# RWKV scan: the triangular solve made ahead of the chunk steps, and the state's product added per direction

## Chip, cores and metric

One core of a Trainium2 chip runs the whole program. The metric is the device time of one execution in microseconds (us); less is better.

## The reference, cut to what matters

The program is two transformer blocks; the second one's later mixer is an RWKV layer that runs forward and backward over 256 context and 512 latent positions with 16 heads of 64:

```python
def _wkv_step(S, inp):
    r_t, w_t, k_t, v_t, a_t, b_t = inp
    sa = jnp.einsum('zbhvk,zbhk->zbhv', S, a_t)
    S = S * w_t[..., None, :] + sa[..., :, None] * b_t[..., None, :] + v_t[..., :, None] * k_t[..., None, :]
    return S, jnp.einsum('zbhvk,zbhk->zbhv', S, r_t)
...
    gate = jax.nn.sigmoid(xg @ g1) @ g2
    return (y.reshape(bsz, n, d) * gate) @ wo
```

The kernel computes the recurrence in chunks of 64 positions. Inside a chunk, the 64 values `sa` depend on each other through a triangular matrix; with X the inverse of (I - that matrix), `U = X (A S + rest)`.

## The kernel before

The program runs in order: the first block, a gMLP layer, a mixture of experts, `rwkv_project` (from about 2585 us), the scan (class `_RwkvScan`, about 2880 to 3600 us), and a second mixture of experts. Only the last part of `rwkv_project` and the scan are touched.

**Project.** `rwkv_project` makes r, k, v and the gate and stores them in DRAM. The gate ends it: a sigmoid (160x512), split into two fp32r halves (L244, L245), times `rw_g2` in 48 matmuls (L266 to L268), eight copies and eight stores to `rw_g`. The scan's first loads come after.

**Scan.** Eight pairs of heads run one after another. A pair has three stretches u of four chunk steps each (u = 0 is the context, u = 1 and 2 the latents), with both directions z side by side in every step. One step is a chain over three engines. TensorE (PE): `ry` = A·S (L2600; L2605 in u = 0). VectorE (DVE): `rz` = ry + rhs (L2609; L2611 copies in the first step, which has no state). PE: `up` = X·rz (L2616). ScalarE (ACT): copy into `UV` (L2620). PE: `sps`, the state's product (L2625). DVE: the new state `S`, one instruction for each direction (L2636; L2634 in the first step). Beside it ACT scales the state (L2643), and PE and ACT finish the output `yn` (L2649, L2653).

**Beside the steps.** `run` calls the generator `scan(p)` under a high priority and fills in work from `beside(p)`, which for the pair after (n = p + 1) and the one after that makes: elementwise operands (`pre`; PE L2309, DVE L2332 to L2365), triangles (PE L2376, DVE `xT` L2381), the store and reload of the 32x32 triangles by DMA (`load_tri`), the forward substitution on GpSimd (POOL; `subst`, 62 instructions at L2420 and L2424), its return by DMA (`back`), the 64x64 inverses from the 32x32 ones (`merge`: DVE transpose `XoP` L2449, PE L2456 and L2471), the products and `rest` (`prep`: PE L2516, L2522, L2531, L2555; masks on DVE), and the finished pair's norm and gate (`out`; bv's product at L2566 is in `prep`). A scheduler orders the instructions of each engine from these priorities, and each engine then runs its list in order: an instruction that waits holds all behind it on its engine.

PSUM has eight banks: two for `ry`, one each for `up` and the state's product, two for `aa`, two for `tp`.

Of the kernel before, what the change touches and what calls it, by code (L numbers as in the profile page):

```python
# [10 lines left out]
F32 = mybir.dt.float32  # L11
# [182 lines left out]
class Kern:  # L194
# [1684 lines left out]
    def rwkv(self):  # L1879
        nc, io = self.nc, self.io  # L1880
        with ExitStack() as c:
            dp = self.pool("rwdram", space=DRAM, ctx=c)
            dr = {n: dp.tile([D, TA if n in "kvq" else T], F32, name=f"rw_{n}") for n in ("r", "k", "v", "q", "g", "y")}
# [29 lines left out]
    def rwkv_project(self, c, R, dr):  # L1913
# [140 lines left out]
        def gates(out):  # L2054
            for (a, b), (ps, _, _) in zip(((0, 128), (128, 160)), out):
                sg = self.wk.tile([P, TA], F32, tag="ksq", name="rwsg", bufs=2)
                nc.scalar.activation(sg[: b - a, :T], ps[: b - a, :], AF.Sigmoid)
                raw = hp.tile([P, KD, P], F32, tag="pw128", name="pw", bufs=3)
                wH = hp.tile([P, KD, P], F32R, tag="pH128", name="pH", bufs=3)
                wL = hp.tile([P, KD, P], F32R, tag="pL128", name="pL", bufs=3)  # L2060
# [3 lines left out]
        gate = []  # L2064
        beside = (s for g in (kk(), thin(5, [([(0, io["rw_g1"][:, a:b])], b - a) for a, b in ((0, 128), (128, 160))], T, gates)) for s in g)
        full(0, io["rw_wr"], "r", T, 2, beside)
        parts = []
        for n, sg, raw, wH, wL in gate:
            H = hp.tile([P, TA], F32R, tag="mH", name="mH", bufs=9)
            L = hp.tile([P, TA], F32R, tag="mL", name="mL", bufs=9)  # L2070
            self.split(H[:n, :T], L[:n, :T], sg[:n, :T])
            self.split(wH[:n], wL[:n], raw[:n])
            parts.append((n, H, L, wH, wL))
        for f in range(KD):
            ps = self.pp.tile([P, 512], F32, tag="mm", name="mmps")
            for i, (n, H, L, wH, wL) in enumerate(parts):
                self.mm3(ps, wH[:n, f], wL[:n, f], H[:n, :T], L[:n, :T], i == 0, i == 1)
            st = hp.tile([P, TA], F32, tag="st", name="st", bufs=3)
            nc.scalar.activation(st[:, :T], ps, AF.Copy)
            nc.sync.dma_start(dr["g"][f * P : (f + 1) * P, :], st[:, :T])  # L2080
# [26 lines left out]
class _RwkvScan:  # L2107
# [3 lines left out]
    NSCAN = 36  # L2111

    def __init__(self, K, c, R, dr):
# [4 lines left out]
        self.pp = _Tagged(K.pool("rwps", space=PSUM, ctx=c), {"ry": 2, "u": 1, "s": 1, "aa": 2, "tp": 2})  # L2118
# [9 lines left out]
    def run(self):  # L2128
# [8 lines left out]
        for p in range(8):  # L2137
            sc = self.scan(p)
            for i in range(self.NSCAN):
                need = {("prep", p, i // 12), ("merge", p), ("out", p - 1) if i >= 12 else ("merge", p)}  # L2140
# [4 lines left out]
                if i % 12 == 11:  # L2145
                    self.marks.add(("scan", p, i // 12))
# [9 lines left out]
    def beside(self, p):  # L2156
# [32 lines left out]
        def triangles():  # L2189
# [4 lines left out]
            if n < 8:  # L2194
# [4 lines left out]

        i, own, ahead = 0, operands(), triangles()  # L2200
# [16 lines left out]
        if n < 8:  # L2217
            mg = self.merge(n)
            while True:
                with self.K.tc.high_priority(offset=400) if n == 7 else ExitStack():  # L2220
# [12 lines left out]
    def setup(self):  # L2233
# [21 lines left out]
        self.X = one("X", 32, 32)  # L2255
        self.lora = [one(f"lora{n}", P) for n in "wa"]
        self.rz = [one(f"rz{i}", 2, P) for i in range(2)]
        for t in self.rz:
            nc.gpsimd.memset(t, 0.0)
# [150 lines left out]
    def subst(self, p):  # L2410

        G, X, Lt = self.nc.gpsimd, self.X, self.Lt
# [72 lines left out]
    def prep(self, p):  # L2485
# [62 lines left out]
        def intra(u, AAk, UV):  # L2548
            ps = self.ps()
            for z in range(2):  # L2550
# [9 lines left out]
                yield 0.85  # L2560
            p4 = ps.rearrange("p (z m f) -> p z m f", z=2, m=2)
            A.activation(UV[64:, :, 0::2, :], p4[64:], AF.Copy)
            A.activation(UV[:64, :, 1::2, :], p4[:64], AF.Copy)

# [16 lines left out]
    def scan(self, p):  # L2581
        nc, L = self.nc, self.cur[p]
        V, A, PE = nc.vector, nc.scalar, nc.tensor
        XT = L["XT"]
        st = sp_ = None
        for u in range(3):
# [3 lines left out]
            for j in range(4):  # L2590
# [4 lines left out]
                rhs, rz = UV[Uh, :, j, :], self.rz[q]  # L2595
                if st is not None:
# [12 lines left out]
                    V.tensor_tensor(rz[Uh], ry[Uh, :256].rearrange("p (z f) -> p z f", z=2), rhs, OP.add)  # L2609
                else:  # L2610
                    V.tensor_copy(rz[Uh], rhs)  # L2611
                yield 1
# [307 lines left out]
```

## Time and profile before

| | us |
|---|---|
| median of three runs | 4190.04 |
| lowest, highest | 4182.6, 4209.11 |
| the profiled execution | 4201.93 |
| its span in the trace | 4200.0 |

The profiled execution lies 11.9 us above the median; sums below are made against it. PE has separate lists of matmuls (PE) and weight loads (PEld); an fp32 matmul is two rows of the trace. PEclk is the granted TensorE clock as a share of 2.4 GHz, so 0.50 is the lower level of 1.2 GHz. A timeline row gives the start, the length from the first start to the last end, the engine, line and operation, and how many instructions ran on end (x); in brackets stands the idle time before it and what ended that.

### The profile page before, as it was taken

What the parts mean: (1) busy time and instruction counts of PE and PEld (TensorE: products, weight loads), DVE (VectorE), ACT (ScalarE), POOL (GpSimd) and SP (SyncE); (2) the same over time, 40 slices, a digit from 0 to 9 for tenths busy, and PEclk for the clock granted to TensorE, in tenths of its full rate; (3) what the DMA queues carried; (4) which work ended last, traced back from release to release, by engine and by line L of the source; (5) the groups of instructions that cost most, each with busy time, mean ns of one, the idle gap of its engine ahead of it and who ended that gap; (6) DMA issues with size and microseconds to landing.
All of it is one profiled execution on the core that took longest, in us unless ns stands there. A gap on an engine that the chain in (4) does not pass through costs nothing. (4 is left out here: it accounts for less than half of the span.)

```text
span 4200.0 us, 56465 instructions
## 1 busy us (share of the span) xinstructions
PE 3774.0 (90%) x22550; PEld 2588.1 (62%) x22550; DVE 1838.8 (44%) x3646; ACT 1322.6 (31%) x2612; POOL 683.8 (16%) x889
## 2 busy tenths in 40 slices
PE   7979999999999979998789997996788899688986
PEld 6747778756777869887333334774667777433332
DVE  3445345565534545334422225445657655511112
ACT  3334224344323433233111113424456555200001
POOL 1002000200201010001100002002555342200001
PEclk9969999999999989999899998997768769799998
DMA  3213553212452322122799996342211212499997
GB/s 110 81 38 117 182 192 105 81 32 76 144 179 82 101 70 68 52 102 79 294 406 391 398 404 236 93 152 66 54 40 43 60 48 79 185 394 415 415 413 306
DMA packets 324825, 711.86 MB, mean 169 GB/s; under 512 B 79616, under 2 KB 251904, under 8 KB 299728
## 3 DMA queue, kind: packets, MB, share of 16 engines
q1 hardware_dynamic: 308704, 658.43, 43.1%
q0 software_dynamic: 15856, 49.79, 3.4%
q8 instruction: 179, 2.93, 0.3%
q14 instruction: 86, 0.70, 0.1%
HBM read 666.64 MB, written 47.55 MB: 170 GB/s over the span
## 5 line engine op out<-in xcount | busy, mean ns | idle before, releaser
L266 PE MATMUL mmps<-xH,wH 128*128 128x512 f32 (+1 forms) x1384 | 552.0, 401 | 11.2 <-ACT xH L359 9.4
L268 PE MATMUL mmps<-xH,wL 128*128 128x512 f32 (+1 forms) x1384 | 543.9, 394 | 2.4 <-DVE wL L245 2.4
L267 PE MATMUL mmps<-xL,wH 128*128 128x512 f32 (+1 forms) x1384 | 544.8, 394 | 0.0
L1488 PE MATMUL bgps<-wg,bxT 128*64 128x512 f32 (+2 forms) x1040 | 471.5, 597 | 0.9 <-issue 0.9
L1489 PE MATMUL bgps<-wu,bxT 128*64 128x512 f32 (+1 forms) x896 | 398.2, 597 | 21.1 <-DMA wu<-in_moe_w_up_dram 20.8
L244 ACT ACTIVATE wH<-wraw 128x512 fp32r<-128x512 f32 (+3 forms) x473 | 265.0, 620 | 481.4 <-PE mmps L267 270.6
L245 DVE TENSOR_TENSOR wL<-wraw,wH 128x512 fp32r<-128x512 f32 (+3 forms) x473 | 328.6, 739 | 193.6 <-ACT wH L244 193.0
L266 PEld LDWEIGHTS mmps<-xH,wH 128*128 128x128 f32 (+1 forms) x1384 | 259.9, 188 | 92.4 <-ACT wH L244 12.4
L268 PEld LDWEIGHTS mmps<-xH,wL 128*128 128x128 f32 (+1 forms) x1384 | 259.9, 188 | 66.1 <-DVE wL L245 3.9
L1505 PE MATMUL byps<-wd,bhT 128*64 128x512 f32 (+2 forms) x1040 | 297.0, 658 | 1.1 <-ACT bhT L1496 1.1
L267 PEld LDWEIGHTS mmps<-xL,wH 128*128 128x128 f32 (+1 forms) x1384 | 260.2, 188 | 59.9 <-issue 1.4
L1488 PEld LDWEIGHTS bgps<-wg,bxT 128*64 128x64 f32 (+2 forms) x1040 | 139.0, 137 | 206.7 <-issue 200.3
L1490 ACT ACTIVATE bh<-bgps 64x512 f32<-64x512 f32 (+2 forms) x65 | 38.3, 590 | 641.2 <-PE bgps L1489 543.0
L1489 PEld LDWEIGHTS bgps<-wu,bxT 128*64 128x64 f32 (+1 forms) x896 | 111.9, 128 | 132.7 <-issue 91.6
L1491 DVE TENSOR_TENSOR bh<-bgps,bh 64x512 f32<-64x512 f32 (+1 forms) x56 | 38.6, 690 | 335.7 <-ACT bh L1490 335.7
L1505 PEld LDWEIGHTS byps<-wd,bhT 128*64 128x64 f32 (+2 forms) x1040 | 87.9, 147 | 157.8 <-issue 152.1
L2420 POOL TENSOR_TENSOR isub<-xT,rwX 96x31 f32<-96x31 f32 (+15 forms) x248 | 140.6, 567 | 262.0 <-DMA xT<-rwd 243.2
L1454 POOL DMA_INDIRECT xg<-hnat,ix x65 | 62.8, 967 | 640.1 <-PE bxps L1476 602.9
L2424 POOL TENSOR_TENSOR rwX<-rwX,isub 96x31 f32<-96x31 f32 (+15 forms) x248 | 155.5, 627 | 19.4
L2807 POOL TENSOR_TENSOR sqs<-sqs,sq 128x512 f32<-128x512 f32 (+1 forms) x60 | 82.3, 1372 | 392.8 <-ACT sq L2800 386.4
L266 PE MATMUL mmps<-mH,pH 128*128 128x512 f32 (+2 forms) x336 | 124.1, 372 | 12.0 <-ACT pH L244 9.1
L532 POOL TENSOR_TENSOR ffng<-ffng,rstd 128x512 f32<-128x512 f32 x44 | 57.8, 1316 | 452.2 <-ACT ffng L531 439.9
(746 smaller groups left out, 7529.6 us busy)
## 6 DMA issues: line engine op xcount, KB each, us to landing
wg<-in_moe_w_gate_dram SPq DMA_DIRECT2D x64, 2048.0 KB, 23.1
wu<-in_moe_w_up_dram SPq DMA_DIRECT2D x61, 2048.0 KB, 20.1
wd<-in_moe_w_down_dram SPq DMA_DIRECT2D x61, 2048.0 KB, 19.2
adaw<-in_ada_w_dram SPq DMA_DIRECT2D x48, 1024.0 KB, 5.0
wraw<-in_ffn_w_gate_dram SPq DMA_DIRECT2D x22, 1024.0 KB, 5.4
wraw<-in_ffn_w_up_dram SPq DMA_DIRECT2D x22, 1024.0 KB, 5.5
wraw<-in_ffn_w_down_dram SPq DMA_DIRECT2D x20, 1024.0 KB, 5.0
wraw<-in_ga_w_in_dram SPq DMA_DIRECT2D x16, 1024.0 KB, 5.5
```

The lines of the kernel that those rows point to most:

```text
L244: self.nc.scalar.activation(H, src, AF.Copy)
L245: self.nc.vector.tensor_tensor(L, src, H.bitcast(F32), OP.subtract)
L266: nc.tensor.matmul(out, lh, rh, start=first, stop=False)
L267: nc.tensor.matmul(out, lh, rl, start=False, stop=False)
L268: nc.tensor.matmul(out, ll, rh, start=False, stop=last)
L1454: self.gathered = self.nc.gpsimd.indirect_dma_start(out=x[:m, :], out_offset=None, in_=hnat, in_offset=bass.IndirectOffsetOnAxis(ap=it, ax ...
L1488: nc.tensor.matmul(og, xT[:, k, :m], wg[:, k, :], start=k == 0, stop=k == KD - 1, skip_group_check=True)
L1489: nc.tensor.matmul(ou, xT[:, k, :m], wu[:, k, :], start=k == 0, stop=k == KD - 1, skip_group_check=True)
L1505: nc.tensor.matmul(o[j], hT[:, k, :m], wd[:, k, j * 512 : (j + 1) * 512], start=k == 0, stop=k == 3, skip_group_check=True)
L2420: G.tensor_tensor(o, Lt[:96, :j, j : j + 1].to_broadcast((96, j, n)), X[:96, j : j + 1, j:].to_broadcast((96, j, n)), OP.mult,)
L2424: G.tensor_tensor(X[:96, :j, j:], X[:96, :j, j:], o, OP.add)
L2807: K.nc.gpsimd.tensor_tensor(self.acc, self.acc, t, OP.add)
```

## The change

`UV` now holds X·rest before the scan reaches it, and `AR` holds X·A in place of A. For that `prep` gets for each u: an identity copied on ACT and eight transposes of `AR` (`L2559`), a DVE copy (L2563), 16 matmuls for X·A (L2577), 16 for X·rest (L2589), two DVE copies into `AR` (L2594) and two ACT copies into `UV`. The part of u = 0 needs the merged X and is placed behind `merge`; those of u = 1 and 2 run during the scan.

A step is then: PE `ry` (L2634, L2639), DVE adds it into `UV`, one instruction for each direction (L2644), PE `sps` (L2649), DVE `S` (L2658, L2660). `up`, `rz` and the copy into `UV` are gone, and the bank of `up` goes to `tp`.

The gate's product leaves `rwkv_project`: the sigmoid itself is stored, and `out(p)` loads it with two pieces of `rw_g2` and makes the product by two fp32 matmuls (L2725, L2726). The substitution of the first pair runs on DVE instead of POOL, ahead of the other filling work.

```diff
-                nc.sync.dma_start(raw[: b - a], io["rw_g2"][a:b, :].rearrange("p (k f) -> p k f", f=P))
-                gate.append((b - a, sg, raw, wH, wL))
...
+                nc.sync.dma_start(dr["g"][a:b, :], sg[: b - a, :T])
...
-        for f in range(KD):
-            ps = self.pp.tile([P, 512], F32, tag="mm", name="mmps")
-            for i, (n, H, L, wH, wL) in enumerate(parts):
-                self.mm3(ps, wH[:n, f], wL[:n, f], H[:n, :T], L[:n, :T], i == 0, i == 1)
...
-    NSCAN = 36
+    NSCAN = 24
...
-        self.pp = _Tagged(K.pool("rwps", space=PSUM, ctx=c), {"ry": 2, "u": 1, "s": 1, "aa": 2, "tp": 2})
+        self.pp = _Tagged(K.pool("rwps", space=PSUM, ctx=c), {"ry": 2, "s": 1, "aa": 2, "tp": 3})
...
+        if n == 0:
+            for _ in inv:
+                pass
+            self.back(0)
+            self.marks.add(("subst", 0))
...
-            mg = self.merge(n)
+            mg = (w for g in (self.merge(n), self.cur[n]["solve"]) for w in g)
...
-        G, X, Lt = self.nc.gpsimd, self.X, self.Lt
+        G, X, Lt = self.nc.gpsimd if p else self.nc.vector, self.X, self.Lt
...
+                    PE.matmul(
+                        ps[64 * (1 - pr) : 64 * (1 - pr) + 64, (2 * z + m) * P : (2 * z + m + 1) * P],
+                        AR[:, 4 * z + j, (1 - pr) if u else 0, :], K.ident, start=True, stop=True, skip_group_check=True,
+                    )
+            V.tensor_copy(An, ps)
...
+                        PE.matmul(
+                            wps[j % 2][64 * h : 64 * h + 64, (2 * z + m) * 64 : (2 * z + m) * 64 + 64],
+                            An[r0 : r0 + 64, (2 * z + m) * P + 64 * h : (2 * z + m) * P + 64 * h + 64],
+                            XT[r0 : r0 + 64, u * 8 + z * 4 + h * 2 + m, :], start=True, stop=True, skip_group_check=True,
+                        )
...
+                        PE.matmul(
+                            ps[r0 : r0 + 64, o : o + 64], XT[r0 : r0 + 64, u * 8 + z * 4 + h * 2 + m, :],
+                            I[r0 : r0 + 64, o : o + 64], start=True, stop=True, skip_group_check=True,
+                        )
+            for q, w in enumerate(wps):
+                V.tensor_copy(AR[:, q::2, (1 - q) if u else 0, :], w[:, :256].rearrange("p (x i) -> p x i", i=64))
...
-                    V.tensor_tensor(rz[Uh], ry[Uh, :256].rearrange("p (z f) -> p z f", z=2), rhs, OP.add)
...
-                            up[Uh, z * P + 64 * h : z * P + 64 * h + 64], XT[:, u * 8 + z * 4 + h * 2 + m, :],
-                            rz[:, z, 64 * h : 64 * h + 64], start=True, stop=True, skip_group_check=True,
...
-                A.activation(rhs, up[Uh, :256].rearrange("p (z f) -> p z f", z=2), AF.Copy)
+                    for z in range(2):
+                        V.tensor_tensor(uv[:, z], ry[Uh, z * P : (z + 1) * P], uv[:, z], OP.add)
...
-        V.tensor_tensor(yT, gt, yT, OP.mult)
+        ps = self.ps()
+        PE.matmul(ps, g2, gt, start=True, stop=False)
+        PE.matmul(ps, g2low, self.glow, start=False, stop=True)
+        V.tensor_tensor(yT, ps, yT, OP.mult)
```

How the lists of the engines change. First PE over two steps of a late stretch, before (`rwups` is `up`, `rwsps` the state's product):

```order
11189 L2600 MATMUL rwryps<-S,ARl 128x128 [waits DVE_49] x2
11190 L2616 MATMUL rwups<-rwrz_19396,rwXT_19389 64x64 [waits DVE_49]
11191 L2616 MATMUL rwups<-rwrz_19396,rwXT_19389 64x64 x3
11192 L2625 MATMUL rwsps<-UV,BKn 64x64 [waits Activation_49]
11193 L2625 MATMUL rwsps<-UV,BKn 64x64 x3
11194 L2649 MATMUL rwryps<-UV,AAr 64x64 x4
```

The same place in the changed kernel, one step (`rwryps` is `ry`; L2528 and L2519 are filling work):

```order
11334 L2634 MATMUL rwryps<-S,ARl 128x128 [waits DVE_49]
11335 L2528 MATMUL rwtpps<-ident,vrev 128x128
11336 L2519 MATMUL rwtpps<-ident,BK 128x128 [waits Activation_49]
11337 L2519 MATMUL rwtpps<-ident,BK 128x128 x3
11338 L2649 MATMUL rwsps<-UV,BKn 64x64 [waits DVE_49]
11339 L2649 MATMUL rwsps<-UV,BKn 64x64
11340 L2519 MATMUL rwtpps<-ident,BK 128x128 [waits Activation_49]
11341 L2649 MATMUL rwsps<-UV,BKn 64x64 [waits DVE_49]
11342 L2649 MATMUL rwsps<-UV,BKn 64x64
11343 L2673 MATMUL rwryps<-UV,AAr 64x64 x4
```

Three waits of PE in a step have become two, each split by direction, with filling work between them.

Then DVE at the end of a steady pair before, around the transpose `XoP`, which waits for two DMAs that bring back the substitution's result:

```order
2309 L2359 TENSOR_TENSOR BK<-km,E_23120 128x4x2x64 [waits DVE_49]
2310 L2365 TENSOR_TENSOR kms<-kms,km 128x256 x2
2311 L2381 TENSOR_TENSOR xT<-rwaaps,rwmask 128x2x128 x2
2312 L2393 SCALAR_TENSOR_TENSOR kms<-inr,pv,kms 128x512 [waits DVE_49]
2313 L2449 STREAM_TRANSPOSE XoP<-rwXT_19388 128x768 [waits DMAHW5_49,DMAHW0_49]
2314 L2381 TENSOR_TENSOR xT<-rwaaps,rwmask 128x2x128 [waits PE_49] x2
2315 L2611 COPY rwrz_19395<-UV 64x256 [waits Activation_49]
```

The same transpose in the changed kernel, in the middle of the pair's steps:

```order
2402 L2644 TENSOR_TENSOR UV<-rwryps,UV 64x128 [waits PE_49]
2403 L2644 TENSOR_TENSOR UV<-rwryps,UV 64x128
2404 L2513 TENSOR_TENSOR AAk<-rwaaps,rwmask 128x256
2405 L2437 STREAM_TRANSPOSE XoP<-rwXT_19290 128x768 [waits DMAHW7_49,DMAHW1_49]
2406 L2660 SCALAR_TENSOR_TENSOR S<-rwsps,P,SP 128x128 [waits DVE_49,PE_49,Activation_49]
2407 L2660 SCALAR_TENSOR_TENSOR S<-rwsps,P,SP 128x128
2408 L2644 TENSOR_TENSOR UV<-rwryps,UV 64x128 [waits PE_49,Activation_49]
2409 L2644 TENSOR_TENSOR UV<-rwryps,UV 64x128
```

`XoP` has moved from behind the last step's addition to a place with four steps and the state of a fifth still behind it; the last `xT` (L2369) stands some 40 rows later.

## Rows read from the trace of the kernel before

**Rows 1.** Timeline of all engines, one quick step, from one rz to the next
```profile
3230.06 0.43 DVE L2609 TENSOR_TENSOR rwrz<-rwryps,UV 64x256 f32<-64x256 f32 x1
...
3230.83 0.68 PE L2616 MATMUL rwups<-rwrz,rwXT 128*64 128x64 f32 x8
...
3231.54 0.38 ACT L2620 ACTIVATE UV<-rwups 64x256 f32<-64x256 f32 x1 [0.51 <-PE rwups L2616]
...
3232.49 0.45 PE L2625 MATMUL rwsps<-UV,BKn 128*64 128x64 f32 x8
...
3232.99 0.61 DVE L2636 SCALAR_TENSOR_TENSOR S<-rwsps,P,SP 128x128 f32<-128x128 f32 x2 [0.82 <-PE rwsps L2625]
...
3233.70 0.71 PE L2600 MATMUL rwryps<-S,ARl 128*128 128x128 f32 x4
...
3234.64 0.41 DVE L2609 TENSOR_TENSOR rwrz<-rwryps,UV 64x256 f32<-64x256 f32 x1
```
**Rows 2.** Stretches: PE, PEld, DVE, ACT, POOL busy (instructions), PEclk, DMA share, GB/s
```profile
3307.00:3355.00 48.00, 41.28 (x492) 33.35 (x492) 36.37 (x101) 35.28 (x79) 17.23 (x29) 0.89 0.21 54
3355.00:3389.00 34.00, 33.48 (x371) 26.30 (x368) 13.66 (x34) 10.98 (x25) 19.44 (x36) 0.50 0.16 36
3389.00:3439.00 50.00, 42.67 (x517) 34.63 (x516) 38.76 (x105) 36.88 (x81) 17.63 (x29) 0.88 0.19 50
3467.00:3594.00 127.00, 121.52 (x1237) 93.75 (x1235) 67.07 (x193) 59.41 (x134) 20.29 (x35) 1.00 0.26 76
```
**Rows 3.** Timeline of DVE around one pair's steps: last rz before, XoP, xT
```profile
3348.76 0.39 DVE L2609 TENSOR_TENSOR rwrz<-rwryps,UV 64x256 f32<-64x256 f32 x1
...
3355.57 0.97 DVE L2449 STREAM_TRANSPOSE XoP<-rwXT 128x768 f32<-128x768 f32 x1
3356.47 0.71 DVE L2381 TENSOR_TENSOR xT<-rwaaps,rwmask 128x256 f32<-128x256 f32 x2
```
**Rows 4.** Timeline of DVE: the same pair's fifth and its last rz
```profile
3397.11 0.43 DVE L2609 TENSOR_TENSOR rwrz<-rwryps,UV 64x256 f32<-64x256 f32 x1
...
3430.80 0.39 DVE L2609 TENSOR_TENSOR rwrz<-rwryps,UV 64x256 f32<-64x256 f32 x1
```
**Rows 5.** Timeline of POOL: first and last operation of one substitution, start of the next
```profile
3284.15 0.25 POOL L2420 TENSOR_TENSOR isub<-xT,rwX 96x31 f32<-96x31 f32 x1 [21.00 <-DMA xT<-rwd]
...
3324.71 0.24 POOL L2424 TENSOR_TENSOR rwX<-rwX,isub 96x31 f32<-96x31 f32 x1
...
3366.82 0.25 POOL L2420 TENSOR_TENSOR isub<-xT,rwX 96x31 f32<-96x31 f32 x1 [37.35 <-DMA xT<-rwd]
```
**Rows 6.** Timeline of POOL: last operation of the first pair's substitution
```profile
2964.53 0.24 POOL L2424 TENSOR_TENSOR rwX<-rwX,isub 96x31 f32<-96x31 f32 x1
```
**Rows 7.** Timeline of DVE in the first pair's start
```profile
2931.36 0.66 DVE L2347 SCALAR_TENSOR_TENSOR bb<-th,inq 128x256 f32<-128x256 f32 x1 [0.56 <-ACT th L2316]
...
2971.43 0.98 DVE L2449 STREAM_TRANSPOSE XoP<-rwXT 128x768 f32<-128x768 f32 x1 [4.63 <-DMA rwXT<-rwd]
2980.90 0.61 DVE L2634 TENSOR_SCALAR S<-rwsps,P 128x128 f32<-128x128 f32 x2 [8.49 <-PE rwsps L2625]
```
**Rows 8.** Timeline of PE: the gate's first and last rows, then the scan's first
```profile
2858.12 1.20 PE L266 MATMUL mmps<-mH,pH 128*128 128x512 f32 x4 [2.92 <-ACT mH L244]
...
2878.64 0.62 PE L268 MATMUL mmps<-mH,pL 32*128 32x512 f32 x1
2888.38 1.22 PE L2309 MATMUL rwtpps<-rw_tw,rwloraw 64*128 64x256 f32 x4 [9.12 <-DMA rwloraw<-in_rw_w_dram]
```
**Rows 9.** Timeline of PE at the full clock: work like that which is added
```profile
3413.22 1.12 PE L2566 MATMUL rwtpps<-kms,rwblk 128*128 128x512 f32 x2
...
3415.13 0.68 PE L2376 MATMUL rwaaps<-ARc,BK 64*64 64x64 f32 x16
3415.74 0.71 PE L2600 MATMUL rwryps<-S,ARl 128*128 128x128 f32 x4
...
3434.98 1.15 PE L2555 MATMUL rwtpps<-UV,AAk 128*64 128x64 f32 x32 [1.48 <-ACT BKn L2532]
```

More of the change, by code (lines that the diff above doesn't have):

```diff
@@ L1882, in rwkv @@
             dp = self.pool("rwdram", space=DRAM, ctx=c)
-            dr = {n: dp.tile([D, TA if n in "kvq" else T], F32, name=f"rw_{n}") for n in ("r", "k", "v", "q", "g", "y")}
+            dr = {n: dp.tile([D, TA if n in "kvq" else T], F32, name=f"rw_{n}") for n in ("r", "k", "v", "q", "y")}
+            dr["g"] = dp.tile([160, T], F32, name="rw_g")
             dr["x"] = dp.tile([P, KD * T], F32, name="rw_x")
@@ L2139, in run @@
             for i in range(self.NSCAN):
-                need = {("prep", p, i // 12), ("merge", p), ("out", p - 1) if i >= 12 else ("merge", p)}
+                need = {("prep", p, i // 8), ("merge", p), ("out", p - 1) if i >= 8 else ("merge", p)}
                 while not need <= self.marks:
@@ L2144, in run @@
                     next(sc)
-                if i % 12 == 11:
-                    self.marks.add(("scan", p, i // 12))
+                if i % 8 == 7:
+                    self.marks.add(("scan", p, i // 8))
                 goal += 100 / self.NSCAN
@@ L2255, in setup @@
         self.X = one("X", 32, 32)
+        low = self.X[96:].rearrange("p s t -> p (s t)")
+        self.glow, self.g2low = low[:, :T], low[:, T:].rearrange("p (n f) -> p n f", f=P)
+        nc.sync.dma_start(self.glow, self.dr["g"][P:, :])
         self.lora = [one(f"lora{n}", P) for n in "wa"]
-        self.rz = [one(f"rz{i}", 2, P) for i in range(2)]
-        for t in self.rz:
-            nc.gpsimd.memset(t, 0.0)
         self.sps = self.ps("s")
@@ L2560, in intra, with solve @@
                 yield 0.85
+            flat = AAk.rearrange("p x m q i -> p (x m q i)")
+            An, I = flat[:, :512], flat[:, 512:]
+            A.activation(I, ps, AF.Copy)
+            ps = self.ps()
+            AR = L["AR"][u]
+            for z in range(2):
+                for j in range(4):
+                    m, pr = j // 2, j % 2
+                    PE.matmul(
[3 more added lines that the diff above has]
+            V.tensor_copy(An, ps)
+            yield 0.6
+            L["solve"] = solve(u, An, I, UV)
+            if u:
+                yield from L["solve"]
+        def solve(u, An, I, UV):
+            XT, AR = L["XT"], L["AR"][u]
+            wps = [self.ps() for _ in range(2)]
+            for z in range(2):
+                for j in range(4):
+                    m, r0 = j // 2, 64 * (1 - j % 2)
+                    for h in range(2):
+                        PE.matmul(
[3 more added lines that the diff above has]
+                        )
+            yield 0.9
+            ps = self.ps()
+            for z in range(2):
+                for h in range(2):
+                    for j in range(4):
+                        m, r0 = j // 2, 64 * (1 - j % 2)
+                        o = (2 * z + m) * P + 64 * h
+                        PE.matmul(
[4 more added lines that the diff above has]
+                V.tensor_copy(AR[:, q::2, (1 - q) if u else 0, :], w[:, :256].rearrange("p (x i) -> p x i", i=64))
             p4 = ps.rearrange("p (z m f) -> p z m f", z=2, m=2)
```

37 lines of the change are left out of this document (10 added, 27 removed).

## The prediction

> **What bounds the kernel now.** I first looked at the 40 slices of the page for the place of the scan, then at the sums over stretches, then at the timelines of DVE, POOL and PE over one steady pair of heads, and last at the start of the scan. PE is the busiest engine in the scan, yet its clock is not steady. A steady pair lasts from one last `rz` to the next, 3348.76 to 3430.80, 82.0 us [rows 3, 4]. In 34 us of that PE runs at 0.50 of its clock and is busy for 33.48: there it is the bound. In the 50 us behind, at a mean of 0.88, it is busy for 42.67, and in the stretch ahead for 41.28 of 48: there it has gaps, and a step's chain over the engines can set the pace [rows 2]. The half clock begins at the change of pairs, where PE turns to many small matmuls of the inverses; how the chip decides the level no row shows.
>
> The chain of a quick step takes 4.58 us: `rz` at 3230.06, `up` .77 later, the copy into `UV` .71 later, `sps` .95 later, `S` .50, `ry` .71, next `rz` .94 [rows 1]. In the second part of a steady pair, the fifth to the last `rz`, 33.69 us hold 7 steps, 4.81 each [rows 4]: near to the chain, so this part is latency. The first part, last `rz` of one pair to the fifth of the next, takes 48.35 us [rows 3, 4], and most of that is PE at half clock.
>
> POOL is far from the path before: a substitution takes 3284.15 to 3324.95, 40.8 us, and POOL then idles for 37.35 us with a wait for the next triangles [rows 5]. The result is asked for by `XoP` only at 3355.57 [rows 3], some 24 us after it has come back.
>
> **The gate and the start.** Removed: PE's gate product, 2858.12 to 2879.26, and 9.12 us of PE waiting for the scan's first loads, so that the scan's first matmul starts at 2888.38 [rows 8]. Afterwards the first loads wait for the store of the sigmoid alone. The sigmoid is done just before 2858; a store that others wait for is not shown alone, but the transfer from the substitution's end, 2964.77, to `XoP`, 2971.43, is two such legs in 6.7 us [rows 6, 7], so one is about 3. Then 9.1 us for the loads: PE starts at about 2870, 18 to 20 us earlier. I take 19. The eight copies and stores hide nothing else there.
>
> Then the first substitution moves to DVE. 62 operations of 31 to 256 columns each: DVE's own rows of 256 columns take .39 to .43 us [rows 4], so the sum is below 27 us, and I take .33 each, 20.5. In DVE's list they lie among 33 operands' operations of the second pair, which start in the trace of before at 2931.36 [rows 7]; at some .5 us each that is 16.5. So the stretch takes about 37 us and `XoP` comes at 2931.4 + 37 + 6.7 = 2975 in the old count, where it now is 2971.43 [rows 7]: 3.6 later. Behind `merge` comes the solution for u = 0 (below, about 3 to 4 us at half clock) before the first `S`. So 7 us of the 19 go back: the start gives 12, with bounds of 3 (27 us for the substitution) and 19.
>
> **A step.** `rz`, `up` and the copy were .77 + .71 + .95 = 2.43 us from add to `sps` [rows 1]; afterwards one hop of DVE to PE, like `rz` to `up`, .77. The chain of a quick step falls from 4.58 to about 2.9. Were every one of the 7 late steps to gain 1.66, that is 11.6 us a pair. That is the gain the change could make, before it is asked what else is late.
>
> **PE's work.** Removed are four `up` matmuls a step; their neighbours of the same shape, 32 rows, take 1.15 us [rows 9], and the 8 of `up` .68 [rows 1], of which about .52 is until the next could start: a pair's twelve, 6.2 us at full clock. Added for each u: eight transposes, 16 rows of the kind that take .18 each with their tail (four in .71) [rows 9], of which pairs go to different halves of the array as at L2555, so about .07 each, 1.1 us; 32 rows for X·A, in quarters like the triangles (16 in .68 [rows 9], so .02 to .04 each), .8; 32 for X·rest, 1.15 by the row of L2555. Together 3.05, for three u 9.2. The gate: two matmuls like L2566, 1.12 with the tail [rows 9], 2.0. So PE has 9.2 + 2.0 - 6.2 = 5 us more a pair at full clock, 2 to 9 by the ends of the transposes' price.
>
> Where it lies matters more. In the half-clock part everything counts twice: the solution of u = 0 (3.9), the transposes for u = 0 and 1 (4.4), half of u = 1 (2), less four `up` steps (4.2 to 4.8): about 5.5 more, 48.35 becomes 54. The late part holds 33.69 x .85 = 28.8 us of PE work now, less 7 x .52, plus u = 2 and the gate, 5: 30.2. So by PE alone the late part can shrink from 33.7 to 30 and no further, and the pair goes to 84. The clock may come out better: PE with fewer gaps in the late part might keep the full level longer. I count nothing for that.
>
> Of the Trainium skill, the page "TensorEngine Tiling (Array Packing)", section "Key Properties", has a rule that speaks against the change: a change of tiling mode drains TensorE, and the solution's small tiles stand among the steps' large ones. The row bears little of it: 16 rows of 64*64 tiles began at 3415.13 and the next rows, of 128*128, at 3415.74, .61 us, where 16 rows at L2555's spacing would take .58 [rows 9]. By the row a switch costs .03 us and some 40 more of them a pair 1.2 us, 8 us in all, so that by the rule the time would be 4185; without it the sum stands as below.
>
> **DVE and the substitution.** This is where I think the step's gain goes. In the changed list `XoP` stands ahead of the state of a step in the middle of the pair, with that state and four steps behind it, where it stood behind the last addition. DVE cannot pass it before the substitution is back. And the next triangles, which start the next substitution, stand behind those steps. So POOL, which had 37 us to spare, closes a ring: triangles to substitution 3357.18 to 3366.82, 9.6 us [rows 3, 5]; substitution 40.8; return 6.7; `XoP` 1.0; a bit over four steps; and from the last addition to the last triangle 8.4 less `XoP`'s 1.0, 7.4 [rows 3]. With steps of 2.9 to 4.8 us, four and a third take 12.5 to 21; I take 3.8, 16.5. Sum 82.0, with ends of 78 and 86.5. The old pair lasted 82.0. The ring therefore gives no gain, whatever the chain of a step would allow, and the waiting DVE holds the masks that feed PE.
>
> DVE's own additions (24 halves of an addition instead of 12 whole ones, three copies of 512 columns, six of 256) are about 6 us a pair; with 38.76 of 50 busy [rows 2] they have room, except behind `XoP`. ACT loses 12 copies of .38 and gains three. The loads for `out` go out long before they are used.
>
> **Sum.** Pairs: ring 82.0, PE 84, against 82.0 now; the late part has slack that overlaps the two, and I take no change. The last two pairs run at the full clock with PE busy for 121.52 of 127 [rows 2]; there `up` of 23 steps goes (12) and one pair's solution and three gates come (9 + 6), against gaps of 5.5 that may close: 0. So 4201.9 - 12 = 4190 for the profiled execution, 4178 against the median of the runs, which lies 11.9 below. I say 4177.
>
> **Rivals.**
> 1. *The chain was the bound and the ring doesn't hold.* If the substitution is back before DVE reaches `XoP`, the late part falls to PE's 30 or, with the clock up longer, below, and the first part stays: a pair of about 72 to 76. For it: POOL's 37 us of idle time; against it, the ring's sum. Seven pairs at -8 with the start's -12: about -68, 4122.
> 2. *The two limits add up: slower.* DVE waits at `XoP`, PE finds no operands and idles; the work it could not do lies at the change of pairs, at half clock, with the 5.5 us added there. A pair is then 82 + 5.5 + 3: seven of them +60, with the start -12: +48, 4238. It decides from the point where `XoP`'s wait on DVE is over 3 us a pair and the first part over 54. For it: PE busy for 33.48 of 34 in that part; against: some fill does go on on PE, and the steps behind `XoP` are quicker.
> 3. *Only the gate counts:* the first substitution costs nothing on DVE and pairs don't move: -19, 4171. It lies within the forecast's range.
>
> **How the numbers follow.** About 1% is what a measurement here can tell from no change. Forecast with the third rival: 0.55, own range 4155 to 4200. First rival 0.25; second 0.20, of which a part ends below +1%. Faster by over 1% (below 4148): 0.27; within 1%: 0.56; slower (above 4232): 0.17. The range reaches into both: 4112 to 4232.
>
> **What would show it.** Right: PE's first scan row some 19 us earlier, counted from the sigmoid; `XoP` on DVE in steady pairs waits for the DMA by 1 to 10 us; POOL's idle time before a substitution falls to below 37 us only if pairs shorten, and the gaps between starts of substitutions stay 78 to 86; the late steps that do not wait take about 3 to 4 us. Wrong: starts of substitutions 70 to 76 apart (first rival), or over 87 (second); a first `S` later than 2971 in the old count; half-clock stretches much shorter or longer than 34 us a pair.

## The result, and the profile after

The changed kernel takes 4236.4 us (median of six runs, 4230.05 to 4246.27), the kernel before 4193.12 (six runs): 1.0109 times as long, interval 1.0086 to 1.0133. The forecast was 4177 in 4112 to 4232: the change is slower, and the time lies just above the range. The profiled execution after took 4230.05 us (span 4228.3), 28 more than the one before. That is less than the 43 between the medians, since one lies at the bottom of its kernel's runs and the other above its median; the traces are used for where time goes, the ratios for how much.

I lined the two traces up by the starts of the state `S` (two rows of the line for each step). First the line's own row of before, then of after (duration min/median/max in ns, first and last start):

```profile
L2636 DVE SCALAR_TENSOR_TENSOR S<-rwsps,P,SP x160: 330/343/353, 2987.9 to 3582.8; 128x128 f32<-128x128 f32 x160
```

```profile
L2658 DVE TENSOR_SCALAR S<-rwsps,P x16: 318/335/351, 2956.6 to 3554.1; 128x128 f32<-128x128 f32 x16
L2660 DVE SCALAR_TENSOR_TENSOR S<-rwsps,P,SP x160: 320/343/353, 2960.0 to 3607.2; 128x128 f32<-128x128 f32 x160
```

The first `S` comes at 2956.6 (before: 2980.90 [rows 7]), 24.3 us earlier; the last 24.4 later. So the eight pairs lose 48.7. Some 4 of the 24.3 lie ahead of the sigmoid (ACT), which both kernels compute: it ends at 2852.91 after and at 2857.07 before, and in the experiments' traces with the new gate anywhere from 2852.7 to 2866.7. So those 4 are taken as spread and not as gain; counted from the sigmoid, the first `S` is 20.1 us earlier. From one pair's first `S` to the next one's (the eighth: to its last `S`), us:

| pair | 0 | 1 | 2 | 3 | 4 | 5 | 6 | 7 |
|---|---|---|---|---|---|---|---|---|
| before | 68.7 | 84.2 | 79.5 | 74.7 | 82.0 | 82.2 | 79.5 | 50.8 |
| after | 89.1 | 94.0 | 82.4 | 84.5 | 84.9 | 76.0 | 86.3 | 53.2 |
| after, XoP and `back` moved (e11) | 77.0 | 82.3 | 81.7 | 81.3 | 84.5 | 78.1 | 75.7 | 55.3 |

Pairs 0 and 1 lose 30 of the 48.7; the steady ones, 2 to 5, lose 9.4 together. Each kernel has one trace, so a look at the others tells what is clear of their spread. Pairs 0 and 1 together take 145 to 153 us in three traces with the old step (before, e3, e12 below) and 176 to 188 in five with the new one (after, e1, e2, e5, e7). Pairs 2 to 5 take 318 to 337 in the former and 321 to 341 in the latter: the loss there is not clear of it.

**The early pairs.** The timeline of DVE after, from the first substitution's end (L2412) on:

```profile
2936.29 0.19 DVE L2412 TENSOR_TENSOR rwX<-rwX,isub 96x31 f32<-96x31 f32 x1
...
2956.64 0.61 DVE L2658 TENSOR_SCALAR S<-rwsps,P 128x128 f32<-128x128 f32 x2 [0.73 <-PE rwsps L2649]
...
2988.41 0.98 DVE L2437 STREAM_TRANSPOSE XoP<-rwXT 128x768 f32<-128x768 f32 x1 [15.19 <-DMA rwXT<-rwd]
...
3098.91 0.42 DVE L2513 TENSOR_TENSOR AAk<-rwaaps,rwmask 128x256 f32<-128x256 f32 x1 [9.43 <-DMA rw_y<-AAk]
...
3517.57 0.98 DVE L2437 STREAM_TRANSPOSE XoP<-rwXT 128x768 f32<-128x768 f32 x1 [6.86 <-DMA rwXT<-rwd]
```

The second pair's `XoP` stands in the middle of the first pair's steps and holds DVE for 15.19 us. Its substitution is not late: it starts on POOL at 2941.1, 15.5 us ahead of the first `S`, where before it started at 2976.7, 4.2 ahead. It is `XoP` that stands early; before, it ran behind the last step, at 3039.5. In pair 1, a mask (L2513) waits 9.43 us for a buffer that the store of y, on SP's queue, has to read. Why that store was late the queue shows (SPq, when each DMA was issued):

```profile
3092.83 0.32 SPq L2419 DMA_DIRECT2D rwd<-rwX  x1
3093.20 0.42 SPq L2691 DMA_DIRECT2D g<-in_rw_g_dram  x1
...
3096.33 0.53 SPq L2729 DMA_DIRECT2D rw_y<-AAk  x1
```

L2419 is the first DMA of `back`; it waits for the substitution, which ended on POOL at 3092.8, and y's store stands behind it. The same queue holds the load of v in pair 0, for which ACT waits 19.5 us, during `XoP`'s wait:

```profile
2980.39 0.31 SPq L2419 DMA_DIRECT2D rwd<-rwX  x1
...
2984.36 0.45 SPq L2273 DMA_DIRECT2D inv<-rw_v  x1
```

The waits of the scan, 2880 to 3660 us (total, times, longest), before and then after:

```profile
ACT vrev L2493 <- DMA inv<-rw_v: 9.6, 1, 9.6
...
DVE XoP L2449 <- DMA rwXT<-rwd: 6.3, 2, 4.6
```

```profile
DVE XoP L2437 <- DMA rwXT<-rwd: 28.9, 3, 15.2
...
ACT vrev L2481 <- DMA inv<-rw_v: 21.0, 2, 19.5
DVE AAk L2513 <- DMA rw_y<-AAk: 17.1, 3, 9.4
```

Of the 28.9 us, 6.80 lie ahead of the first step; the other two waits are those of pairs 0 and 6 above.

**A steady pair.** `XoP` does not wait there, but by little: POOL ends at 3258.64 and `XoP` runs at 3267.23, 8.6 us behind; in pairs 2 to 5 it is 8.6 to 9.6 us, and where `XoP` waited, in pairs 0 and 6, it came 8.1 and 7.5 behind. The ten intervals from `S` to `S` of pair 4, then the gap to the next pair:

| | 1 | 2 | 3 | 4 | 5 | 6 | 7 | 8 | 9 | 10 | gap |
|---|---|---|---|---|---|---|---|---|---|---|---|
| before | 6.1 | 7.5 | 6.8 | 9.2 | 5.5 | 5.1 | 4.3 | 4.1 | 5.2 | 5.0 | 23.0 |
| after | 4.4 | 3.5 | 2.8 | **21.9** | 4.1 | 3.2 | 7.8 | 6.3 | 4.5 | 3.1 | 23.4 |

Steps of about 3 us, as forecast, where nothing disturbs them; two of 6 to 8, and one hole. The first four intervals sum to 29.6 before and 32.6 after, the other six to 29.2 and 29.0. The pair in stretches (columns as in [rows 2]; the hole is the second row, the whole pair the last), and pair 4 of before under it:

```profile
3306.60:3317.20 10.60, 7.70 (x103) 5.93 (x103) 8.24 (x24) 6.58 (x15) 9.50 (x15) 0.84 0.11 37
3317.20:3339.10 21.90, 13.24 (x146) 9.73 (x146) 19.01 (x51) 10.08 (x19) 19.70 (x29) 0.69 0.05 14
3339.10:3368.10 29.00, 25.58 (x274) 19.52 (x274) 15.19 (x41) 13.16 (x32) 4.37 (x11) 0.82 0.19 45
3368.10:3391.50 23.40, 21.99 (x483) 18.46 (x481) 15.94 (x40) 13.41 (x30) 4.89 (x12) 1.00 0.31 82
3306.60:3391.50 84.90, 68.52 (x1002) 53.64 (x1002) 58.38 (x154) 43.24 (x94) 38.47 (x65) 0.84 0.18 46
```

```profile
3288.00:3370.00 82.00, 74.76 (x856) 59.66 (x856) 49.99 (x133) 46.26 (x103) 36.77 (x63) 0.73 0.19 46
```

Pair 4 of before ran at a mean granted clock of 0.73, pair 4 of after at 0.84. Pair 3 of before, at 0.83, is nearer:

```profile
3213.30:3288.00 74.70, 67.34 (x856) 53.99 (x856) 52.48 (x133) 46.67 (x104) 44.20 (x74) 0.83 0.21 51
```

At about the same clock, with PE busy for about as long, the pair after is 10 us longer. Over pairs 2 to 5 the mean is 0.76 before and 0.84 after, so a loss in the steady pairs may be hidden by a higher clock; no run separates the two.

In the hole PE is busy for 13.24 of 21.90 us, DVE for 19.01. What PE waits for, and what DVE does meanwhile:

```profile
3324.37 0.61 PE L2634 MATMUL rwryps<-S,ARl 128*128 128x128 f32 x4
...
3333.71 1.01 PE L2649 MATMUL rwsps<-UV,BKn 128*64 128x64 f32 x8 [7.69 <-DVE UV L2644]
```

```profile
3317.18 0.59 DVE L2660 SCALAR_TENSOR_TENSOR S<-rwsps,P,SP 128x128 f32<-128x128 f32 x2
...
3325.13 2.12 DVE L2322 TENSOR_TENSOR_SCAN cs<-rwreset,sg 128x256 f32<-128x256 f32 x2
...
3333.36 0.29 DVE L2644 TENSOR_TENSOR UV<-rwryps,UV 64x128 f32<-64x128 f32 x1
...
3334.21 2.75 DVE L2712 TENSOR_SCALAR AAk<-AAk,grs 128x64 f32<-128x64 f32 x8
...
3339.12 0.61 DVE L2660 SCALAR_TENSOR_TENSOR S<-rwsps,P,SP 128x128 f32<-128x128 f32 x2
```

The hole has three parts. From the state to 3324.98, 7.2 us, the solution of u = 1 is finished (its last copy into `UV` ends on ACT at 3322.43) and PE works down filling that stands ahead of `ry`. `ry` is done at 3324.98 and added at 3333.36: 8.4 us in which DVE works down filling (elementwise operands of a later pair, the norm of the pair before) that stands ahead of the addition in its list. `sps` is done at 3334.72 and read at 3339.12: 4.4 more behind filling. Before, the same kinds of rows (operands at L2347 to L2359, the norm at L2677) stood between the steps' rows from 3298 to 3328, and the steps there took 5 to 9 us each.

### The profile page after: what moved, and what is told of

Its sections match the earlier page's. It is cut to its first block, busy times and chain, and to the rows that moved or that the text cites. A ratio compares the mean times of both kernels' runs of the same rounds, so it can differ in the third digit from the quotient of the medians.

```text
span 4228.3 us, 58812 instructions
## 1 busy us (share of the span) xinstructions
PE 3721.1 (88%) x23686; PEld 2553.7 (60%) x23686; DVE 1885.6 (45%) x3858; ACT 1292.5 (31%) x2528; POOL 638.9 (15%) x823
## 5 line engine op out<-in xcount | busy, mean ns | idle before, releaser
L2408 POOL TENSOR_TENSOR isub<-xT,rwX 96x31 f32<-96x31 f32 (+15 forms) x217 | 123.5, 569 | 270.7 <-DMA xT<-rwd 254.2
L2837 POOL TENSOR_TENSOR sqs<-sqs,sq 128x512 f32<-128x512 f32 (+1 forms) x60 | 82.3, 1371 | 393.3 <-ACT sq L2830 386.9
L2412 POOL TENSOR_TENSOR rwX<-rwX,isub 96x31 f32<-96x31 f32 (+15 forms) x217 | 131.1, 604 | 17.0
L1495 PEld LDWEIGHTS bhps<-ident,bh 64*128 64x128 f32 (+2 forms) x260 | 36.0, 208 | 144.3 <-DVE bh L1491 144.3
## 6 DMA issues: line engine op xcount, KB each, us to landing
wd<-in_moe_w_down_dram SPq DMA_DIRECT2D x61, 2048.0 KB, 19.5
```

The costliest lines, as they stand in the source:

```text
L2408: G.tensor_tensor(o, Lt[:96, :j, j : j + 1].to_broadcast((96, j, n)), X[:96, j : j + 1, j:].to_broadcast((96, j, n)), OP.mult,)
L2412: G.tensor_tensor(X[:96, :j, j:], X[:96, :j, j:], o, OP.add)
L2837: K.nc.gpsimd.tensor_tensor(self.acc, self.acc, t, OP.add)
```

## The experiments

Ratios are to the kernel before on the same chip, with 95% intervals. The medians of before beside them run from 4196.63 to 4201.97, where the result had 4193.12; so a gain over after can be up to 17 us larger by the ratios than by the medians; both are given where it matters.

**1. Filling held back (e1), one addition for both directions (e2), the gate alone on the kernel before (e3).** e1 in `beside`, before the next operands are taken; e2 in the step; e3 is the diff's gate and nothing else.

```diff
-            if i % 2 == 0:
+            if (p < 0 or ("prep", p, 1) in self.marks and (p == 0 or ("out", p - 1) in self.marks)):
```
```diff
-                    for z in range(2):
-                        V.tensor_tensor(uv[:, z], ry[Uh, z * P : (z + 1) * P], uv[:, z], OP.add)
+                    V.tensor_tensor(uv, ry[Uh, :256].rearrange("p (z f) -> p z f", z=2), uv, OP.add)
```

> The changed kernel, but the next-but-one pair's operands are not emitted between the running pair's until out of the pair before is emitted, so that in DVE's list 4 fills stand before the fifth step's addition in place of 16; XoP then stands behind the last addition. List theory (the fifth step waits 22 us because its addition stands behind filling on DVE): the stretch from the fourth to the fifth state falls from 22 to 24 us to under 13, pairs from 85 to 72 to 78, time 4150 to 4190. PE theory (the added matmuls and the half clock): filling only moves, pairs stay at 82 to 88, time 4215 to 4250. Ring theory (the substitution is late): XoP no longer holds steps, but triangles come later, pairs 80 to 84, time 4200 to 4220.

> The changed kernel with one addition for both directions (64x256) instead of two. If the split costs DVE time and puts filling between the halves: 96 steps less up to 0.3 us, time 4205 to 4225. If the split lets PE start sooner on the first direction: slower by 5 to 20, 4240 to 4256. List theory: the list of DVE around the fifth step is nearly the same, so within 10 of 4236.

> The kernel before with the gate's part of the change alone. The prediction's term: 19 us earlier start, less some 2 us a pair on PE: ratio to before 0.995 to 0.999, time 4173 to 4190. If PE's added fp32 matmuls and loads cost more than they free (PE theory): 4193 or more.

e1: 4236.77, 1.0084 [1.0057, 1.0110]. Pair 4's fourth interval falls to 6.3, but the sixth grows to 12.6 and the gap from 23.4 to 30.5: 82.4. The hole moved, the pair stayed; and it stayed although DVE is busy for only 52.72 us of it. e2: 4234.14, 1.0085 [1.0052, 1.0119]: the split into directions costs or gives nothing that shows. e3: 4199.1, 0.9997 [0.9978, 1.0017]: its first `S` comes at 2963.1, 17.8 earlier, its last at 3581.0, 1.8 earlier (2980.9 and 3582.8 before):

```profile
L2620 DVE TENSOR_SCALAR S<-rwsps,P x16: 342/348/352, 2963.1 to 3528.7; 128x128 f32<-128x128 f32 x16
L2622 DVE SCALAR_TENSOR_TENSOR S<-rwsps,P,SP x160: 319/344/354, 2968.9 to 3581.0; 128x128 f32<-128x128 f32 x160
```

The start's gain is real (21.6 us, counted from the sigmoid), and 16 us go in the pairs; the ratio agrees that nothing is left.

**2. Is it POOL? The substitution cut to 3 of its 31 rows for pairs 1 to 7, in after (e4) and in before (e8); the first one back on POOL (e5).** Both e4 and e8 leave work out.

```diff
+            if p and j % 8:
+                yield 0
+                continue
```
```diff
-        G, X, Lt = self.nc.gpsimd if p else self.nc.vector, self.X, self.Lt
+        G, X, Lt = self.nc.gpsimd, self.X, self.Lt
```

> The changed kernel with the POOL substitution cut to 3 of its 31 rows for pairs 1 to 7 (leaves out most of the substitution). Ring theory: XoP waits for nothing, pairs fall below 78, time under 4190. Sharing theory (DVE's operations beside POOL take twice as long, as 2.12 us for two scans against 1.25): the same rows before the fifth addition take 6 us less, time 4190 to 4215. List theory alone: the fifth step still stands behind 20 rows, 4215 to 4236.

> The kernel before with the POOL substitution cut to 3 of its 31 rows for pairs 1 to 7 (leaves out most of the substitution). If the substitution costs the changed kernel something that it did not cost the kernel before (sharing, ring): 4185 to 4200 here against the 73 us that the same cut gave there. If it costs both alike: 4120 to 4145.

> The changed kernel with the first pair's substitution on POOL again. Head-of-line theory for the first pair (XoP of the second pair waits 15 us on DVE in mid-steps, since the second substitution starts only when the first has left X): the first state comes 5 to 10 us later, and XoP's wait in the first pair grows, so the time stays or rises, 4236 to 4255. Theory that the DVE substitution displaces work that lay hidden beside POOL: the second pair's first state comes 10 to 16 us earlier than 3045.7 and the time is 4215 to 4226.

e4: 4163.43, 0.9912 [0.9879, 0.9945], 73 less than after's median; pairs of 73 to 76 in the middle, the hole still 24. e8: 4129.29, 0.9831 [0.9784, 0.9878], 67 less than before on that chip. So the substitution costs the old kernel as much, though in the pair read for the forecast its result had waited there for 24 us: what it costs is mostly not the ring, and not the change's own. Two things moved with it. DVE's busy time falls, in pair 4 from 58.38 to 51.02 us in after (below) and from 49.99 to 45.85 in before; and the granted clock rises, from 0.84 to 0.89 and from 0.73 to 0.98. How much of the 73 and 67 us goes by each, no run separates.

```profile
3258.20:3334.20 76.00, 66.95 (x1004) 52.26 (x1004) 51.02 (x153) 43.37 (x94) 4.79 (x8) 0.89 0.21 51
```

By these pairs, of the 8.4 us by which DVE's work rose some 5 are the change's own (51.02 against 45.85), and the rest is that more of it now lies beside POOL's. e5: 4230.66, 1.0078 [1.0047, 1.0109]: pair 0 falls from 89.1 to 76.0, pair 1 rises to 100.2 with the mask's wait, and the first `S` comes at 2961.6. The wait mostly changes its place.

**3. Where `XoP` stands (e6, e9), `back`'s queue (e10), both (e11), and the gate made as before (e7).** e6: `merge` emitted later; e9: the same, and tied behind the last addition by a copy of one element; e10: `back`'s DMAs on POOL's queue; e7: after with the gate's part undone.

```diff
+        while n < 8 and ("scan", p, 2) not in self.marks:
+            yield next(wo, None)
```
```diff
+        if p:
+            nc.vector.tensor_copy(XoP[0:1, 0, 0:1], self.cur[p - 1]["UV"][2][0:1, 0, 3, 0:1])
```
```diff
-        nc.sync.dma_start(d2, self.X[:96])
+        nc.gpsimd.dma_start(d2, self.X[:96])
...
-                nc.sync.dma_start(
+                nc.gpsimd.dma_start(
```

> The changed kernel with merge of the next pair (and with it XoP) emitted only after the running pair's last step; DVE's list then has 4 rows in place of 16 before the fifth step's addition, and XoP stands behind the last addition. Head-of-line theory (XoP in mid-steps holds DVE in the first and the last pairs, the filling ahead of the fifth step in all): the first pair's hole of 27 us goes to under 12, pairs to 74 to 80, time 4180 to 4210. Sharing theory (what counts is DVE's own work, made 7 to 8 us a pair longer beside POOL): pairs stay at 82 to 85, only the first and the seventh pair gain, time 4215 to 4228. No effect of the place of XoP: 4230 to 4245.

> The changed kernel with the gate's product back in the project stage (undoes that part alone). The gate alone on the kernel before brought the first state 18 us forward and gave 16 back over the eight pairs. If the same holds here: within 5 of 4236. If the fifth step's hole hides the gate's added work: later by 12 to 20, 4248 to 4256. If the gate's loads and matmuls lengthen the hole: 4215 to 4230.

> The changed kernel with the next pair's XoP tied behind the running pair's last addition (one copied element makes it depend on it) and merge emitted after the steps: XoP stands where it stood in the kernel before. Head-of-line theory (DVE is held in mid-steps by XoP, 29 us in all in three pairs, and 48 in seven where merge was late): XoP's waits for the DMA fall to under 10 us, no hole of over 20 us in the first pair, time 4195 to 4220. If XoP's place is not what counts (the filling's own chain sets the pair): 4230 to 4250.

> The changed kernel with the five DMAs that bring the substitution back issued by POOL itself instead of SP, so that SP's later DMAs (the store of y, the load of v) no longer stand behind a wait for POOL. SP theory (DVE waits 17 us for AAk's store, ACT 30 us for v, both behind that wait): these two waits fall to under 10 us together, the second pair shortens by 8 to 15 us, time 4215 to 4228. If POOL's own issue costs more than SP's: XoP comes 1 to 3 us later in each pair, 4240 to 4260.

> e9 and e10 together. If both are head-of-line costs of the substitution and add: 4180 to 4205, the pairs behind the second 80 to 84. If one hides the other: as the better of the two.

> The kernel before with the same five DMAs issued by POOL: there AAk's store is not waited for and v costs 10 us once, so SP's wait should hide nothing: 4190 to 4205. If the time falls below 4180, what e10 shows is no cost of the change.

e6: 4256.74, 1.0132 [1.0088, 1.0175]. A miss that shows much: the scheduler put `XoP` behind the eighth step in pairs 1 to 5 (the fourth in pair 0, the tenth in pair 6), and it waits in every one of the seven:

```profile
DVE XoP L2439 <- DMA rwXT<-rwd: 48.4, 7, 15.4
```

e7: 4263.34, 1.0154 [1.0110, 1.0199]; first `S` 2981.5, last 3633.9. The scan's part of the change alone is 67 us behind before on that chip; the gate, worth nothing there, gives the changed kernel 27 by the medians and 19 by the ratios, whose intervals overlap; the traces give 25 at the first `S` and 27 at the last. And 2981.5 against 2980.90 [rows 7] (126.7 and 123.8 us behind the sigmoid) says that the first substitution on DVE and the solution of u = 0 cost the first `S` at most 3.

e9: 4223.12, 1.0051 [1.0027, 1.0074]; e10: 4221.89, 1.0034 [1.0013, 1.0055]; e11: 4207.49, 1.0021 [0.9996, 1.0047]. The waits of e9, then of e10:

```profile
ACT vrev L2485 <- DMA inv<-rw_v: 20.8, 2, 19.5
...
DVE XoP L2441 <- DMA rwXT<-rwd: 6.9, 1, 6.9
...
DVE AAk L2517 <- DMA rw_y<-AAk: 5.5, 3, 2.9
```

```profile
DVE XoP L2437 <- DMA rwXT<-rwd: 20.7, 4, 9.7
```

e9 takes the two waits of `XoP` in the pairs away and most of that for y's store, and leaves the load of v: its pair 0 is 97.8 us, longer than after's, since DVE now waits 15.0 us there for a `UV` that stands on ACT behind v (a miss: no hole of over 20 us was expected there). e10 takes both waits behind `back` away, v and y, and that of `XoP` in pair 0; `XoP` waits 9.7 in pair 1 instead. The two waits of pair 0 lie over one another, so only both edits open it. The gains over after are 13, 15 and 29 us by the medians for e9, e10 and e11, and 24, 31 and 37 by the ratios, of 43 to 46 that the change lost; the interval of e11 holds 1, so what is left cannot be told from nothing. e11's pairs stand in the table above: pairs 0 and 1 fall from 183.1 to 159.3, the middle ones stay near 82. The same queue in the kernel before (e12) gives 4198.61, 0.9988 [0.9958, 1.0019]: nothing, so this is a cost of the change. With `XoP` at the end of the pair in e11 the ring of the forecast is far from closed (POOL ends at 3238.3, `XoP` comes at 3267.5), and the pair is no shorter.

**4. What fills the steady pair: the late solution left out (e13 on after, e14 on e11), the gate's matmuls left out (e15 on e11), a higher priority for the scan (e16, offset 2000 instead of 400), `out` behind all of `prep` (e17, on e11).** e14 has both edits of e11; its expectation names the queue wrongly.

```diff
+            if u:
+                p4 = ps.rearrange("p (z m f) -> p z m f", z=2, m=2)
+                A.activation(UV[64:, :, 0::2, :], p4[64:], AF.Copy)
+                A.activation(UV[:64, :, 1::2, :], p4[:64], AF.Copy)
+                return
```
```diff
-        ps = self.ps()
-        PE.matmul(ps, g2, gt, start=True, stop=False)
-        PE.matmul(ps, g2low, self.glow, start=False, stop=True)
-        V.tensor_tensor(yT, ps, yT, OP.mult)
+        V.tensor_tensor(yT, gt, yT, OP.mult)
```

```diff
-                with self.K.tc.high_priority(offset=400):
+                with self.K.tc.high_priority(offset=2000):
```
```diff
-            if p > 0:
-                yield from self.out(p - 1)
-                self.marks.add(("out", p - 1))
...
                 yield from self.gen
                 self.marks.add(("prep", p, 2))
+            if p > 0:
+                yield from self.out(p - 1)
+                self.marks.add(("out", p - 1))
```

> The changed kernel without the solution for u = 1 and 2 (leaves out the transposes, the products and the copies of these two stretches; u = 0 keeps its own): the steps are as short, and the latents' fifth step waits for no solution. Solve theory (the solution of the next stretch, a chain over PE, DVE and ACT, stands on the steps' path and gives their gain back): pairs fall from 82 to 85 to 72 to 77, time 4160 to 4195. Filling theory (the chain of the filling sets the pair, with or without the solution): pairs stay at 80 to 84, time 4215 to 4235.

> The same on the kernel in which XoP stands behind the last addition (e9; the DMAs are SP's). Solve theory: 4150 to 4185; filling theory: 4205 to 4225, as e9.

> e11 without the two gate matmuls in out (leaves out the gate's product: the loaded 128x512 tile multiplies instead). They stand in the hole before the ninth step, 2.0 us each at the half clock, with the wait for them: solve theory and filling theory alike say 3 to 5 us a pair where the hole is the bound: 4170 to 4185. If the hole hides them: 4200 to 4210.

> e11 with the steps' priority offset raised from 400 to 2000 instructions, which spreads the filling otherwise in DVE's list (11 rows before the fifth addition and 18 before the ninth, in place of 4 and 15). If only the place of the block changes: within 10 of 4207. If more blocks ahead of additions cost: 4215 to 4240.

> e11 with out of the pair before emitted after all of prep, so that the solution of u = 2 no longer stands behind out's norm and gate: 12 rows in place of 15 before the ninth addition, and out's rows move to the change of pairs. If out ahead of the solution costs: the hole of 19 us falls to under 12, pairs from 82 to 74 to 78, time 4160 to 4185, below the kernel before. If the filling's amount counts and not its place: within 12 of 4207.

e13: 4206.22, 1.0039 [1.0017, 1.0061], 30 less than after. But it is not its steady pairs that gain, which were expected at 72 to 77: pairs 2 to 5 take 81 to 84 us at a clock of 0.71 to 0.77 (after: 76 to 85 at 0.83 to 0.84), and pairs 0, 1, 6 and 7 gain all of it. e14: 4160.4, 0.9910 [0.9880, 0.9939], 47 less than e11, some 6 us a pair; its pair 3 and that of e11:

```profile
3191.40:3266.60 75.20, 64.50 (x844) 49.26 (x844) 57.31 (x147) 42.76 (x92) 42.02 (x70) 0.84 0.19 52
```

```profile
3201.90:3283.20 81.30, 67.09 (x1002) 52.90 (x1002) 57.12 (x154) 43.16 (x94) 42.03 (x70) 0.83 0.18 48
```

The pair is 6.1 us shorter with only 2.6 less of PE work and as much on DVE: on this kernel the late solution costs as a chain, not as work. In e11 one sees it ahead of the ninth step, the first of u = 2 (timeline of DVE):

```profile
3231.47 0.61 DVE L2664 SCALAR_TENSOR_TENSOR S<-rwsps,P,SP 128x128 f32<-128x128 f32 x2 [0.26 <-PE rwsps L2653]
...
3236.41 1.91 DVE L2716 TENSOR_SCALAR AAk<-AAk,grs 128x64 f32<-128x64 f32 x8
...
3245.57 0.69 DVE L2567 COPY AAk<-rwtpps 128x512 f32<-128x512 f32 x1 [2.93 <-PE rwtpps L2563]
...
3247.27 0.74 DVE L2598 COPY ARl<-rwtpps 128x256 f32<-128x256 f32 x2
...
3249.65 0.50 DVE L2648 TENSOR_TENSOR UV<-rwryps,UV 64x128 f32<-64x128 f32 x2 [1.63 <-ACT UV L2600]
```

That addition needs u = 2's solved `AR` and `UV`; the solution is made only now, behind the norm and output of the pair before. e15: 4188.32, 0.9986 [0.9963, 1.0008], 19 less than e11 by the medians and 15 by the ratios, whose intervals overlap: about 2 us a pair for two matmuls. e16: 4208.23, 1.0027 [0.9999, 1.0054]: no difference. e17: 4200.55, 1.0003 [0.9970, 1.0035], 7 less than e11, inside the intervals: the holes fall from 16 to 21 us to 9 to 14, and the gap between pairs grows from 25 to 30 to 40.

No version that computes everything beats the kernel before.

## Why the prediction was wrong, step by step

- **The gate and the start**: sign right, size too small. PE's first scan row now stands at 2861.32 (before: 2888.38 [rows 8]), with about the same wait for the loads. Counted from the sigmoid, as the forecast's own sign asks, that is 22.9 us earlier where 19 were forecast: it starts 8.4 us behind the sigmoid, where the sum had 12 for a store and a load one after the other.

```profile
2861.32 1.23 PE L2297 MATMUL rwtpps<-rw_tw,rwloraw 64*128 64x256 f32 x4 [10.05 <-DMA rwloraw<-in_rw_w_dram]
```

  Of the 7 us that substitution and solution should have taken back, 3 were lost at the first `S` (e7). The term was 20, not 12.
- **A step**: right. Undisturbed steps take 2.7 to 3.5 us, where 2.9 was forecast.
- **PE's work**: half right. PE is not the bound: it is busy for 68.52 of 84.90 us, where 84 of PE's pair was forecast. Its work at half clock did not double the first part, since the granted clock rose: the change of pairs ran at 0.67 before and at 1.00 after. The forecast counted nothing for that. The drain at a change of tiling mode, which was weighed at 8 us, no run isolates.
- **DVE and the substitution**: the outcome of 82 us for a steady pair was nearly right, its reason was not, and that is luck. The ring closes with a room of some 2 us at most, where a wait of 1 to 10 was forecast, so its sum was near; but it does not set the pair, for e11 opens it by some 20 us without a gain. What the intervals show in its place is the filling: "with 38.76 of 50 busy they have room" was wrong. DVE rises from 49.99 to 58.38 us a pair, and faster steps leave no waits to fill, so a block of that work stands ahead of ready additions. That its amount sets the pair is not shown: e1 and e17 move the block and the pairs stay on average, e1 with only 52.72 us of DVE, and e14 is shorter with as much DVE as e11.
- **The sum is where the forecast failed**: "Pairs: ring 82.0, PE 84, against 82.0 now; ... I take no change" was worked out from a steady pair and applied to all, and the others' waits were put at nothing. Pairs 0, 1 and 6 lose 37 of the 49 us. Waits that hold a whole queue fall there: `XoP` on DVE and `back` on SP, both for POOL. The two edits of e11 bring back 29 of the 43 us by the medians and 37 of 46 by the ratios, and the same queue in the old kernel (e12) brings nothing. That SP would hold y's store and the load of v behind `back` was not weighed at all; in the text only `XoP`'s place was.
- **The rivals**: the second gave 4238, and the time is 4236, but by another way: it had every steady pair at 90 with PE at half clock to blame. What is shared is `XoP` holding DVE, in the steps of two pairs instead of seven. The first fell: where the ring is open (e11), the steady pairs stay at 78 to 85; runs of pairs of 72 to 76 exist only with work left out (e4, e14), single ones elsewhere. The third's sum fell too: the gate gives 0 alone and 19 to 27 with the rest.
- **Open**: what holds a steady pair at 82. e14 and e15 say, on e11, that the added late solution (6 us) and the gate's product (2) give back much of what the steps gain; e13 on after does not say so. A rival is untested: the granted clock differs from kernel to kernel (0.73 to 0.98 in pair 4) and may give and take what the chain does not. Why the rest cannot close up when the list is reordered, no run settled. Nor was a list tried in which every filling instruction is placed by hand.

## What to carry to other kernels

Before a chain is shortened, ask what used to fill its waits: sum that work over a period, and look where in the in-order list it will stand; here it stood in a block of 22 us. For each instruction that waits for a far engine, a DMA issue too, look at the first and the last period apart from the steady one, and name what is queued behind it. And take a gain at the start as gained only when the end has moved: here 18 us at the first step were 2 at the last.

## What the runs showed that was not expected

- The same pair does not get the same clock. Two pairs of before with the same number of PE rows ran at 0.83 (74.70 us) and 0.73 (82.00), pair 4 of after at 0.84. Whether the clock makes the pair shorter or another thing does both, no run separates; the higher clock made the forecast's doubled first part too dear.
- Some DVE operations are longer while POOL runs the substitution. In the changed kernel the pair of scans on DVE takes 1.25 us at 3278.32, when POOL is idle (it waits until 3300.86), and 2.12 at 3325.13, within a substitution:

```profile
3278.32 1.25 DVE L2322 TENSOR_TENSOR_SCAN cs<-rwreset,sg 128x256 f32<-128x256 f32 x2
```

```profile
3300.86 0.25 POOL L2408 TENSOR_TENSOR isub<-xT,rwX 96x31 f32<-96x31 f32 x1 [37.56 <-DMA xT<-rwd]
```

  The Trainium skill, "Trainium Architecture — The Big Picture", section "What this means for kernel authors", states that on the engines' side of SBUF only the port pair shared by DVE and GpSimd contends, and that it is an exclusive lock. The trace agrees in direction, with .87 us on this operation. In the same stretches the product L2336, both of whose operands are in SBUF, takes 420 ns with POOL idle and 834 ns within the substitution (medians), while the mask L2513 (419 and 411 ns) and the state L2660 (347 and 342), which read one operand from PSUM, are no longer. e4 and e8 put what 28 of the 31 rows cost a whole run, by this and every other way, at 73 and 67 us, nearly alike in the two kernels.
